# The last stage of a two-layer encoder trunk: the residual made token-major by 32-row reads and VectorE transposes instead of TensorE products with the identity

## The chip, the cores and the metric

The kernel runs on one core of a Trainium2 chip, in one launch. The metric is the device time of that launch in microseconds (us). The median of three runs of the kernel before is 1172.42 us (1171.95 to 1172.59). The profile shown below comes from one further execution, which took 1172.3 us; its profiled span is 1170.3 us, so some 2.0 us of an execution lie around the span.

## The reference

The reference is a trunk of two layers over 512 tokens of width 1024, in float32. Each layer is a token mixer, an output projection and a residual, then a gated MLP with a causal convolution, and a residual again. The change concerns only the very end: the down projection of the second layer's MLP (width 2816), its residual, and the final norm.

```python
def rmsnorm(x, g):
    x32 = x.astype(jnp.float32)
    y = x32 * lax.rsqrt(jnp.mean(x32 * x32, axis=-1, keepdims=True) + EPS)
    return (y * g.astype(jnp.float32)).astype(x.dtype)

def conv_ffn(h, w_up, conv_w, conv_b, w_down):
    u, g = jnp.split(h @ w_up, 2, axis=-1)
    g = causal_dwconv(g, conv_w, conv_b)
    return (jax.nn.silu(g) * u) @ w_down
...
for l in range(DEPTH):
    ...
    x = x + conv_ffn(rmsnorm(x, norm_ffn_g[l]), ffn_w_up[l], ffn_conv_w[l], ffn_conv_b[l], ffn_w_down[l])
return rmsnorm(x, final_g)
```

## The kernel before

**Layout.** Activations are kept feature-major: a tile has 128 features as partitions and the 512 tokens along the free axis, so the residual is eight tiles `xT[j]` of 128 x 512. Every float32 product is computed as three matmuls of rounded parts (`mm3`, lines 201 to 203): high by high, high by low, low by high. `split` (lines 145 and 146) makes the parts: ScalarE copies the rounded high part, VectorE subtracts to get the low part.

**The second MLP.** `ChannelMixer.tiles` walks over the 22 tiles of the hidden width. In each step it projects, convolves, gates, and `keep` stores the hidden tile as a pair `(hi, lo)`. The down projection of the first 16 hidden tiles is done inside these steps and added onto the residual in DRAM (`xspill`) by accumulating DMAs on the GpSimd queue. The last six hidden tiles (16 to 21) are left for the last stage. The steps are written in regions of `tc.manual_schedule`, in which TensorE, ScalarE and VectorE each issue their instructions in the written order; an instruction outside a region may be put anywhere between them by the scheduler.

**The last stage** (lines 1578 to 1657, outside any region). `channel_mixer` runs the steps and then `reload_x`, which issues eight reads of 128 x 512 (256 KB, rows of 2 KB) from `xspill` on the SyncE queue into the tiles `fh` and `fl`. The output must be token-major, 128 tokens as partitions, so here the hidden tile is the stationary operand: for each half `hf` of the 1024 output columns, for each pair `u` of hidden tiles (three pairs) and each of four token tiles `T`, TensorE runs 2 x 3 matmuls of 128 x 512 into one PSUM bank per `T`. `ws[u]` is the split pair of weights for `(hf, u)`, loaded into one of three `wr` buffers and split into one of three blocks `wh`/`wl`; the blocks of half 1 reuse those of half 0 when TensorE is through with them. In half 1 the token tiles come in groups: 0 and 1 together, then 2, then 3 in two pieces of 256 columns.

Between half 0 and half 1 stands `token_major(T, hf)`, eight times: four TensorE transposes of 128 x 128 (products with the identity `ident`, line 1590) turn a 128-token column block of four `xT` tiles into one PSUM bank, and a ScalarE copy (line 1592) brings it to SBUF as `xt[T][hf]`. Then `V.tensor_add` (line 1652) adds the product, `add_squares` sums the squares on ScalarE (line 1605), half 0 is multiplied by the final gain (line 1655), and `final_norm(T)` (lines 1607 to 1623) computes the root on ScalarE (line 1610), refines it on VectorE (1611 to 1614), scales both halves (1619 on ScalarE, 1620 on VectorE) and stores them (1621 on the SyncE queue, 1623 on ScalarE's).

The pool tag `pt` has two buffers of 10 KB per partition; in the second MLP they hold the raw weights and the weight sums of the steps (`ChannelMixer.buffers`).

Of the kernel before, what the change touches and what calls it, by code (L numbers as in the profile page):

```python
# [13 lines left out]
ALU = mybir.AluOpType  # L14
# [45 lines left out]
def trunk(  # L60
# [83 lines left out]
    def split(hi, lo, src, on_act=True, pinned=False):  # L144
        high = A.copy(hi, src) if on_act else V.tensor_copy(hi, src)  # L145
        low = V.tensor_tensor(out=lo, in0=src, in1=f(hi), op=ALU.subtract)  # L146
        if pinned:
            pin(high)
            pin(low)
# [3 lines left out]
    def load(src, a, b, extra=None):  # L153
        n = b + (extra.shape[-1] if extra is not None else 0)
        raw = sb("wr", [P, D])[:, : a * n].rearrange("p (a b) -> p a b", a=a)
        if isinstance(src, list):
            for i, one in enumerate(src):
                nc.sync.dma_start(raw[:, i, :], one)
        else:
            loads.append(nc.sync.dma_start(raw[:, :, :b], src))  # L160
        if extra is not None:
            nc.sync.dma_start(raw[:, :, b:], extra)
        return raw
# [28 lines left out]
    def weights(*args):  # L192
        return parts(load(*args))

    def rows(w, c0, n, k0=0, k1=None):
        k1 = k1 if k1 is not None else w.shape[0] // P
        return w[k0 * P : k1 * P, c0 : c0 + n].rearrange("(k p) c -> p k c", p=P)

    def mm3(o, lh, ll, rh, rl, first, last, more=False):

        nc.tensor.matmul(o, lh, rh, start=first, stop=False, skip_group_check=more)  # L201
        nc.tensor.matmul(o, lh, rl, start=False, stop=False, skip_group_check=more)  # L202
        nc.tensor.matmul(o, ll, rh, start=False, stop=last, skip_group_check=more)  # L203
# [537 lines left out]
    class ChannelMixer:  # L741
# [841 lines left out]
    for hf in range(2):  # L1583
        G.dma_start(fgb[hf], bass.AP(tensor=final_g.tensor, offset=final_g.offset + hf * S, ap=[[0, P], [1, S]]))
    xt = [[None] * 2 for _ in range(TT)]

    def token_major(T, hf):
        tp = ps("tr")
        for i in range(4):
            nc.tensor.transpose(tp[:, i * P : (i + 1) * P], xT[4 * hf + i][:, T * P : (T + 1) * P], ident)  # L1590
        xt[T][hf] = sb("u", [P, S])
        A.copy(xt[T][hf], tp)

    sums = [[] for _ in range(TT)]

    def add_squares(T, t):

        if len(sums[T]) == 1:
            V.tensor_scalar(sums[T][0], sums[T][0], 4.0 / D, 4 * EPS, op0=ALU.mult, op1=ALU.add)
        elif sums[T]:  # L1600
# [4 lines left out]
        A.activation(sq[:, : t.shape[-1]], t, AF.Square, accum_out=sums[T][-1])  # L1605

    def final_norm(T):
        v, r, t = small(1), small(1), small(1)
        first, second = sums[T]
        A.activation(r, second, AF.Sqrt, scale=4.0 / D, bias=first)  # L1610
        V.scalar_tensor_tensor(v, second, -4.0 / D, first, op0=ALU.mult, op1=ALU.subtract)
        V.reciprocal(r, r)
        V.scalar_tensor_tensor(t, r, v, r, op0=ALU.mult, op1=ALU.mult)
        V.scalar_tensor_tensor(r, t, 3.0, r, op0=ALU.add, op1=ALU.mult)
        step = S if T < TT - 1 else MEM
        for c in range(0, S, step):
            a, b = (t[:, c : c + step] for t in xt[T])
            last = c + step == S
            A.activation(a, a, AF.Copy, scale=r)
            V.scalar_tensor_tensor(b, b, r, fgb[1][:, c : c + step], op0=ALU.mult, op1=ALU.mult)  # L1620
            nc.sync.dma_start(out[T * P : (T + 1) * P, S + c : S + c + step], b)
            if last:
                nc.scalar.dma_start(out[T * P : (T + 1) * P, :S], xt[T][0])

    hid = channel_mixer(mixer)
    n = LAST // 2
    for hf in range(2):
        os_ = [ps(t) for t in (("mm", "mm", "mm", "sc") if hf == 0 else ("sc", "sc", "tr", "tr"))]
        ws = [None] * n
        groups = [(range(TT), (slice(0, S),))]  # L1630
        if hf:

            groups = [((0, 1), (slice(0, S),)), ((2,), (slice(0, S),)), ((3,), (slice(0, MEM), slice(MEM, S)))]
        for Ts, pieces in groups:
            for c in pieces:
                if c.start:
                    os_[Ts[0]] = ps("mm")
                for u in range(n):
                    if ws[u] is None:
                        k0 = FT - LAST + 2 * u  # L1640
                        ws[u] = weights(rows(ffn_w_down[1], hf * S, S, k0, k0 + 2), 2, S)
                    wh, wl = ws[u]
                    for T in Ts:
                        for i in range(2):
                            k = 2 * u + i
                            lh, ll = (t[:, T * P : (T + 1) * P] for t in hid[k])
                            mm3(os_[T][:, c], lh, ll, wh[:, i, c], wl[:, i, c], k == 0, k == LAST - 1)
                if not hf:
                    for i in range(KT):
                        token_major(i % TT, i // TT)  # L1650
                for T in Ts:
                    V.tensor_add(xt[T][hf][:, c], xt[T][hf][:, c], os_[T][:, c])
                    add_squares(T, xt[T][hf][:, c])
                    if hf == 0:
                        V.tensor_mul(xt[T][0], xt[T][0], fgb[0])
                    elif c.stop == S:
                        final_norm(T)


# [44 lines left out]
```

## Time and profile before

| what | value |
|---|---|
| runs, median of 3 (lowest, highest) | 1172.42 us (1171.95, 1172.59) |
| the profiled execution | 1172.3 us, span 1170.3 us, granted TensorE clock 0.999 |
| TensorE matmul busy | 1159.8 us, 99% of the span |
| VectorE busy | 992.1 us, 85% |
| ScalarE busy | 748.4 us, 64% |
| GpSimd busy | 151.6 us, 13% |
| HBM traffic | 149 GB/s over the span |

Times in the trace are microseconds from the start of the span. A row of the timeline gives the start, the duration, the engine, the line of the kernel, the operation, what it writes and reads by the program's names with the shape, how many were merged, and in brackets the idle time before it with what ended it. PE is TensorE's matmuls, PEld its weight loads, DVE VectorE, ACT ScalarE, SPq and ACTq the DMA queues of SyncE and ScalarE. The ends of matmuls are modelled and overlap the next one, so the pace of matmuls is read from the distance of their starts; on VectorE too an instruction overlaps the next by a little.

### The profile page before, as it was taken

The numbers are of one execution on the slowest core, as the hardware profiler recorded it, in microseconds if no ns is written. First come the engines' busy times: TensorE is split into PE (matmuls) and PEld (weight loads), VectorE is DVE, ScalarE is ACT, GpSimd is POOL, SyncE is SP. The second block draws the span as 40 slices with busy tenths as digits, with TensorE's granted clock in tenths as the row PEclk, the third lists the DMA queues.
The fourth block names the chain that finished last, engine by engine and source line by source line (L and its number), as shares of the span: only waits on it lengthen the run. The fifth ranks groups of instructions, "written<-read, shape, count | busy, mean of one in ns | idle before, by whom it ended". The sixth has DMA issues, their size and how long they took to land.

```text
span 1170.3 us, 19339 instructions
## 1 busy us (share of the span) xinstructions
PE 1159.8 (99%) x7221; PEld 1035.7 (88%) x7221; DVE 992.1 (85%) x1776; ACT 748.4 (64%) x1347; POOL 151.6 (13%) x254
## 2 busy tenths in 40 slices
PE   9999999999999999999999999999999999999997
PEld 9988888888999999999888888778899999999986
DVE  6777688779999988888798888898999998998865
ACT  6548677657766655555666667676766765556645
POOL 1211101000122222111020000101010111111100
PEclk9999999999999999999999999999999999999999
DMA  8745325244478888776573313335445677777661
GB/s 286 225 111 138 91 55 153 68 141 139 130 162 195 195 193 202 181 170 140 151 217 110 91 54 96 106 89 176 122 149 153 143 156 177 175 178 171 135 163 72
DMA packets 204784, 171.27 MB, mean 146 GB/s; under 512 B 9256, under 2 KB 177934, under 8 KB 204690
## 3 DMA queue, kind: packets, MB, share of 16 engines
q1 hardware_dynamic: 184946, 123.93, 36.3%
q0 software_dynamic: 19168, 45.06, 19.3%
q8 instruction: 56, 0.92, 0.3%
q10 hardware_dynamic: 576, 1.05, 0.2%
q14 instruction: 38, 0.31, 0.1%
HBM read 133.09 MB, written 40.85 MB: 149 GB/s over the span
## 4 chain that ended last, share of the span: by engine, by line
PE 95%; ACT 2%; DVE 2%; DMA 0%; issue 0%; SPq 0%; POOL 0%; POOLq 0%; DVEq 0%
PE pmm L201 18%; PE pmm L202 18%; PE pmm L203 18%; PE ptr L202 6%; PE ptr L201 6%; PE ptr L203 6%; PE psc L203 5%; PE psc L202 5%; PE psc L201 5%; PE psc L620 2%; PE ptr L1526 1%; PE ptr L1547 1%; PE ptr L1548 1%; PE ptr L689 0%; DMA u<-in_mem_dram 0%; PE pmm L511 0%
## 5 line engine op out<-in xcount | busy, mean ns | idle before, releaser
L201 PE MATMUL pmm<-u,wh 128*128 128x256 f32 (+1 forms) x992 | 334.7, 338 | 0.2 <-ACT u L145 0.2
L203 PE MATMUL pmm<-u,wl 128*128 128x256 f32 (+1 forms) x992 | 332.0, 335 | 0.0
L202 PE MATMUL pmm<-u,wh 128*128 128x256 f32 (+1 forms) x992 | 331.8, 334 | 0.0
L146 DVE TENSOR_TENSOR wl<-wr,wh 128x1024 fp32r<-128x1024 f32 (+4 forms) x166 | 186.1, 1121 | 67.4 <-ACT wh L145 66.9
L145 ACT CAST wh<-wr 128x1024 fp32r<-128x1024 f32 (+4 forms) x166 | 160.5, 969 | 68.0 <-PE pmm L202 30.0
L203 PEld LDWEIGHTS pmm<-u,wl 128*128 128x128 f32 x992 | 186.3, 188 | 18.8
L201 PEld LDWEIGHTS pmm<-u,wh 128*128 128x128 f32 x992 | 186.4, 188 | 16.8 <-ACT u L145 1.0
L202 PEld LDWEIGHTS pmm<-u,wh 128*128 128x128 f32 x992 | 186.5, 188 | 16.3 <-DVE u L146 0.5
L201 PE MATMUL ptr<-u,wh 128*128 128x512 f32 x272 | 106.5, 391 | 0.0
L202 PE MATMUL ptr<-u,wh 128*128 128x512 f32 x272 | 106.3, 391 | 0.0
L203 PE MATMUL ptr<-u,wl 128*128 128x512 f32 x272 | 105.8, 389 | 0.0
L145 ACT CAST fh<-pt 128x512 fp32r<-128x512 f32 x120 | 74.8, 625 | 34.5 <-DVE pt L1052 33.1
L201 PE MATMUL pmm<-u,fh 128*128 128x256 f32 x320 | 88.9, 278 | 0.0
L203 PE MATMUL pmm<-u,fl 128*128 128x256 f32 x320 | 88.6, 277 | 0.0
L974 ACT COPY t<-pmm 128x256 f32<-128x256 f32 x120 | 45.1, 376 | 67.9 <-PE pmm L203 67.9
L202 PE MATMUL pmm<-u,fh 128*128 128x256 f32 x320 | 88.5, 277 | 0.0
L146 DVE TENSOR_TENSOR fl<-pt,fh 128x512 fp32r<-128x512 f32 x120 | 82.2, 687 | 3.1
L763 DVE SCALAR_TENSOR_TENSOR t<-t,cols,t 128x511 f32<-128x511 f32 x88 | 65.9, 749 | 7.3 <-ACT t L770 5.8
L201 PE MATMUL psc<-u,wh 128*128 128x256 f32 (+1 forms) x208 | 63.2, 304 | 0.0
L203 PE MATMUL psc<-u,wl 128*128 128x256 f32 (+1 forms) x208 | 63.0, 303 | 0.0
L202 PE MATMUL psc<-u,wh 128*128 128x256 f32 (+1 forms) x208 | 62.9, 302 | 0.0
L201 PEld LDWEIGHTS pmm<-u,fh 128*128 128x128 f32 x320 | 60.1, 188 | 2.2 <-ACT t L974 0.7
(360 smaller groups left out, 2638.2 us busy)
## 6 DMA issues: line engine op xcount, KB each, us to landing
wr<-in_ffn_w_up_dram SPq DMA_DIRECT2D x46, 512.0 KB, 8.9
pt<-in_ffn_w_up_dram SPq DMA_DIRECT2D x40, 512.0 KB, 8.0
wr<-in_ffn_w_down_dram SPq DMA_DIRECT2D x32, 512.0 KB, 5.4
wr<-in_a_w_in_dram SPq DMA_DIRECT2D x20, 512.0 KB, 3.9
xspill<-bias POOLq DMA_DIRECT2D x32, 256.0 KB, 6.8
without_row<-bias POOLq DMA_DIRECT2D x24, 256.0 KB, 4.2
wr<-in_w_kv_dram SPq DMA_DIRECT2D x12, 512.0 KB, 3.8
without_row<-t POOLq DMA_DIRECT2D x24, 256.0 KB, 4.2
```

The costliest lines, as they stand in the source:

```text
L145: high = A.copy(hi, src) if on_act else V.tensor_copy(hi, src)
L146: low = V.tensor_tensor(out=lo, in0=src, in1=f(hi), op=ALU.subtract)
L201: nc.tensor.matmul(o, lh, rh, start=first, stop=False, skip_group_check=more)
L202: nc.tensor.matmul(o, lh, rl, start=False, stop=False, skip_group_check=more)
L203: nc.tensor.matmul(o, ll, rh, start=False, stop=last, skip_group_check=more)
L620: nc.tensor.matmul(o, a, b, start=first and i == 0, stop=i == 1)
L763: V.scalar_tensor_tensor(acc[:, n:], src[:, : S - n], self.fw[:, c * FT + j : c * FT + j + 1], acc[:, n:], op0=ALU.mult, op1=ALU.add,)
L974: A.copy(o, r[:, :H])
L1526: nc.tensor.transpose(tp[:, b * P : (b + 1) * P], es[T, h][:, b * P : (b + 1) * P], ident)
L1547: nc.tensor.matmul(o2[:, s * P :], w, hi_at(pts[h], s, s, TT - s), start=s == 0, stop=False)
L1548: nc.tensor.matmul(o2[:, s * P :], w, lo_at(pts[h], s, s, TT - s), start=False, stop=s == TT - 1)
```

## The change

- `reload_x` of the last stage is replaced by `load_quadrants`: two tiles `xq[hf]` in the `pt` buffers, each filled by four reads. A read takes 512 channels by 128 tokens and places them on 32 partitions: partition `32 b + p`, block `f`, column `t` holds channel `32 f + p` of the half and token `128 b + t`. A read has 512 runs of 512 bytes, 256 KB in all; there are eight, as there were eight before.
- `token_major(T, hf)` becomes one VectorE transpose of 128 x 512, which turns each 32 x 32 block by itself, and writes `xt[T][hf]` in SBUF. Its source takes every fourth column of `xq[hf]`. So the token tile `T` now holds the tokens `4 m + T`, with `m` the partition. No transposes on TensorE and no ScalarE copies remain.
- To match, `keep` orders the columns of the last six hidden tiles by `(T, m)`: both instructions of `split` read the source with a step of four elements. `out_rows` stores to rows `4 m + T`.
- The last stage is put in a region of `tc.manual_schedule`, with a written order: half 0 with `u` outermost; the weights of half 1 are split right after each `u` of half 0; the eight VectorE transposes stand after the split of `ws[0]` and ahead of that of `ws[1]`. The first two token tiles' additions of half 0 stand ahead of the split of `ws[2]`. In half 1 the order is `finished` of tiles 0 and 1, `root` of both, `norm_rows` of both, then tile 2, and `norm_rows(2)` behind the addition of the first piece of tile 3.
- The raw weights of half 1 and the eight reads stand in one order on the SyncE queue: weights 0, weights 1, the eight reads, weights 2.
- `final_norm` is cut into `root` and `norm_rows`; the small scaling of the first sum of squares moves ahead of half 1.

```diff
         def keep(self, t):
             hi, lo = sb("u", [P, S], F32R), sb("u", [P, S], F32R)
-            split(hi, lo, t)
+            if self.l and len(self.hid) >= FT - LAST:
+
+                a, b = (w.rearrange("p (T m) -> p T m", T=TT) for w in (hi, lo))
+                split(a, b, t.rearrange("p (m T) -> p T m", T=TT))
+            else:
+                split(hi, lo, t)
...
-    def channel_mixer(mixer):
+    def channel_mixer(mixer, reload=reload_x):
         mixer.tiles()
-        reload_x()
+        reload()
...
+    B = 32
+    xq = []
+
+    def load_quadrants():
+
+        for hf in range(2):
+            xq.append(sb("pt", [P, 5 * S])[:, : 4 * S].rearrange("p (f t) -> p f t", t=P))
+            for b in range(4):
+                block = xspill[4 * hf][:, b * P :]
+                src = bass.AP(tensor=block.tensor, offset=block.offset, ap=[[S, B], [B * S, 16], [1, P]])
+                tc.keep_in_program_order(nc.sync.dma_start(xq[hf][b * B : (b + 1) * B], src))
+
+    def out_rows(T, c0, n):
+        return out.rearrange("(m t) c -> t m c", t=TT)[T][:, c0 : c0 + n]
 
     def token_major(T, hf):
-        tp = ps("tr")
-        for i in range(4):
-            nc.tensor.transpose(tp[:, i * P : (i + 1) * P], xT[4 * hf + i][:, T * P : (T + 1) * P], ident)
         xt[T][hf] = sb("u", [P, S])
-        A.copy(xt[T][hf], tp)
+        block = xq[hf].rearrange("p f (c t) -> p f c t", t=TT)[:, :, :, T]
+        V.transpose(xt[T][hf].rearrange("p (f c) -> p f c", c=B), block)
...
+    def raw_weights(hf, u):
+        k0 = FT - LAST + 2 * u
+        return load(rows(ffn_w_down[1], hf * S, S, k0, k0 + 2), 2, S)
+
+    def reload():
+        ws.extend(parts(raw_weights(0, u)) for u in range(n))
+        for u in range(n):
+            raws.append(raw_weights(1, u))
+            pin(loads[-1])
+            if u == 1:
+                load_quadrants()
...
+    with tc.manual_schedule(engines=ORDERED):
+        os_ = [ps(t) for t in ("mm", "mm", "mm", "sc")]
+        for u in range(n):
+            multiply(os_, range(TT), whole, u)
+            if u == n - 1:
+                for T in range(2):
+                    finished(os_[T], T, 0, whole)
+            ws[u] = parts(raws[u])
+            if not u:
+                for i in range(2 * TT):
+                    token_major(i % TT, i // TT)
+        for T in range(2, TT):
+            finished(os_[T], T, 0, whole)
+        for T in range(TT):
+            V.tensor_mul(xt[T][0], xt[T][0], fgb[0])
+            V.tensor_scalar(sums[T][0], sums[T][0], 4.0 / D, 4 * EPS, op0=ALU.mult, op1=ALU.add)
+        os_ = [ps(t) for t in ("sc", "sc", "tr", "tr")]
+        for u in range(n):
+            multiply(os_, (0, 1), whole, u)
+        for step in (finished_whole, root, norm_rows):
+            for T in range(2):
+                step(T)
+        for u in range(n):
+            multiply(os_, (2,), whole, u)
+        finished_whole(2)
+        root(2)
+        for c in (slice(0, MEM), slice(MEM, S)):
+            if c.start:
+                os_[3] = ps("mm")
+            for u in range(n):
+                multiply(os_, (3,), c, u)
+            finished(os_[3], 3, 1, c)
+            if not c.start:
+                norm_rows(2)
+        root(3)
+        norm_rows(3)
```

`multiply` is the loop of `mm3` over the given token tiles for one `u`; `finished` is the addition and `add_squares`.

More of the change, by code (lines that the diff above doesn't have):

```diff
@@ L1605, in add_squares, with root @@
         A.activation(sq[:, : t.shape[-1]], t, AF.Square, accum_out=sums[T][-1])
-    def final_norm(T):
-        v, r, t = small(1), small(1), small(1)
+    roots = [None] * TT
+    def root(T):
+        v, r = small(1), small(1)
         first, second = sums[T]
@@ L1611, in final_norm, with norm_rows @@
         V.scalar_tensor_tensor(v, second, -4.0 / D, first, op0=ALU.mult, op1=ALU.subtract)
+        roots[T] = v, r
+    def norm_rows(T):
+        (v, r), t = roots[T], small(1)
         V.reciprocal(r, r)
@@ L1620, in final_norm @@
             V.scalar_tensor_tensor(b, b, r, fgb[1][:, c : c + step], op0=ALU.mult, op1=ALU.mult)
-            nc.sync.dma_start(out[T * P : (T + 1) * P, S + c : S + c + step], b)
+            nc.sync.dma_start(out_rows(T, S + c, step), b)
             if last:
-                nc.scalar.dma_start(out[T * P : (T + 1) * P, :S], xt[T][0])
-    hid = channel_mixer(mixer)
+                nc.scalar.dma_start(out_rows(T, 0, S), xt[T][0])
     n = LAST // 2
[L1627 to L1657, printed above, removed]
```

19 lines of the change are left out of this document (16 added, 3 removed).

## The prediction

> **What bounds the kernel now.** I read the page's first lines and its chain, then the timeline of each engine from 1120 us to the end.
>
> ```profile
> PE 1159.8 (99%) x7221; PEld 1035.7 (88%) x7221; DVE 992.1 (85%) x1776; ACT 748.4 (64%) x1347; POOL 151.6 (13%) x254
> ...
> PE 95%; ACT 2%; DVE 2%; DMA 0%; issue 0%; SPq 0%; POOL 0%; POOLq 0%; DVEq 0%
> ```
>
> TensorE is the bound: 95% of the chain is matmuls. So work taken off TensorE is worth its time, until another engine sets the end. The place of the change in TensorE's timeline:
>
> ```profile
> 1141.82 0.40 PE L203 MATMUL psc<-wh,u 128*128 128x512 f32 x1
> 1142.06 1.04 PE L1590 MATMUL ptr<-ident,fh 128*128 128x128 f32 x8
> 1142.85 0.48 PE L201 MATMUL psc<-wh,u 128*128 128x512 f32 x1
> ...
> 1154.54 0.39 PE L201 MATMUL ptr<-wh,u 128*128 128x512 f32 x1
> ...
> 1158.62 0.28 PE L201 MATMUL ptr<-wh,u 128*128 128x256 f32 x1
> ...
> 1160.78 0.28 PE L201 MATMUL pmm<-wh,u 128*128 128x256 f32 x1
> ...
> 1162.82 0.28 PE L203 MATMUL pmm<-wh,u 128*128 128x256 f32 x1
> ```
>
> The first row is the last matmul of half 0, the last row the last of half 1. Token tile 2 is the 18 matmuls from 1154.54 to 1158.62, so a 128x512 matmul takes a pace of 4.08 / 18 = 0.227; the first piece of tile 3 gives 2.16 / 18 = 0.120 for 128x256. The transposes (L1590) stand among the matmuls of tiles 0 and 1 of half 1. What they bring to the other engines:
>
> ```profile
> L1592 ACT COPY u<-ptr 128x512 f32<-128x512 f32 x8 | 4.5, 588 | 0.4 <-PE ptr L1590 0.3
> ...
> L1590 PE MATMUL ptr<-ident,fh 128*128 128x128 f32 x16 | 2.3, 276 | 0.1
> ```
>
> VectorE around it, and ScalarE's cast of the last weights:
>
> ```profile
> 1132.69 1.23 DVE L146 TENSOR_TENSOR wl<-wr,wh 128x1024 fp32r<-128x1024 f32 x1 [0.26 <-ACT wh L145]
> 1137.90 1.23 DVE L146 TENSOR_TENSOR wl<-wr,wh 128x1024 fp32r<-128x1024 f32 x1 [3.98 <-ACT wh L145]
> 1143.34 1.23 DVE L146 TENSOR_TENSOR wl<-wr,wh 128x1024 fp32r<-128x1024 f32 x1 [4.22 <-ACT wh L145]
> 1144.48 1.88 DVE L1652 TENSOR_TENSOR u<-u,pmm 128x512 f32<-128x512 f32 x3
> ...
> 1149.80 0.69 DVE L1655 TENSOR_TENSOR u<-u,bias 128x512 f32<-128x512 f32 x1 [0.34 <-ACT t L1605]
> ...
> 1150.47 0.68 DVE L1655 TENSOR_TENSOR u<-u,bias 128x512 f32<-128x512 f32 x1
> ```
> ```profile
> 1142.26 1.05 ACT L145 CAST wh<-wr 128x1024 fp32r<-128x1024 f32 x1 [4.40 <-PE psc L203]
> ```
>
> VectorE idles 4 us twice during half 0. Three 128x512 operations in a row take 1.88, so each comes 0.60 behind the one before ((1.88 - 0.68) / 2); a 128x1024 one takes a pace of 1.14 (1143.34 to 1144.48); a multiplication by the gain with its small operation 0.67 (1149.80 to 1150.47).
>
> **The change part by part.**
>
> *The 32 transposes leave TensorE.* Without them half 1 begins 0.227 behind the row at 1141.82, at 1142.05. Tiles 0 to 2 are 54 x 0.227 = 12.24, so tile 3 begins at 1154.29 and not at 1158.62: 4.33 us gained. This contains the waits between transposes and copies too. Eight ScalarE copies go (4.5 us); they were beside the matmuls and are counted at nothing more.
>
> *Eight VectorE transposes come.* No row shows one. The nearest is the 128x512 operation at a pace of 0.60 with contiguous operands. The source here takes every fourth element; if that halves the reading, the nearest row is the one with twice the elements, 1.14. Below 0.60 a transpose could only help, and it would not show, as the sum will say. I take 0.60, since the element count is the same, and keep 1.14 for a rival. They stand behind the low part of ws[0] (1132.69 + 1.14 = 1133.83) and end at 1133.83 + 8 x 0.60 = 1138.63. Behind them in VectorE's written order: the low part of ws[1] to 1139.77 (TensorE wants it after 12 matmuls of half 1, at 1144.77), the first two additions to 1140.97 with ScalarE's squares to about 1141.8, the cast of ws[2] at 1142.26 as before (it waits for half 0 to end), its low part from 1143.34 to 1144.48 (wanted at 1142.05 + 24 x 0.227 = 1147.5), two additions to 1145.68, four gain pairs of 0.67 to 1148.36. Tile 0 of half 1 is complete at 1142.05 + 29 x 0.227 + 0.39 = 1149.0. So all of it fits. The reserve is small: 0.44 until the squares push the cast, 0.64 ahead of tile 0, and about 0.8 between tiles 0 and 1: 1.9 us together.
>
> *The written order of the tail.* Before, the tail ran like this:
>
> ```profile
> 1153.38 0.69 DVE L1652 TENSOR_TENSOR u<-u,psc 128x512 f32<-128x512 f32 x1 [2.17 <-PE psc L203]
> ...
> 1156.47 0.16 DVE L1612 RECIPROCAL s<-s 128x1 f32<-128x1 f32 x1 [0.97 <-ACT s L1610]
> ...
> 1157.11 0.75 DVE L1620 SCALAR_TENSOR_TENSOR u<-u,s,bias 128x512 f32<-128x512 f32 x1
> 1157.78 0.15 DVE L1611 SCALAR_TENSOR_TENSOR s<-s,s 128x1 f32<-128x1 f32 x1
> ...
> 1160.97 0.42 DVE L1652 TENSOR_TENSOR u<-u,ptr 128x256 f32<-128x256 f32 x1 [0.92 <-PE ptr L203]
> 1161.31 0.15 DVE L1611 SCALAR_TENSOR_TENSOR s<-s,s 128x1 f32<-128x1 f32 x1
> ...
> 1163.13 0.42 DVE L1652 TENSOR_TENSOR u<-u,pmm 128x256 f32<-128x256 f32 x1 [0.29 <-PE pmm L203]
> ```
> ```profile
> 1154.11 0.63 ACT L1605 ACTIVATE t<-u 128x512 f32<-128x512 f32 x1 [3.73 <-DVE u L1652]
> ...
> 1154.85 1.28 ACT L1610 ACT_TABLE_LOAD   x1
> 1156.14 0.29 ACT L1610 ACTIVATE s<-s,s 128x1 f32<-128x1 f32 x1
> ```
>
> The last addition (1163.13) followed the last matmul at once. Steps read from these rows: addition to square 0.73, square to the next on ScalarE 0.74, table load 1.29, root to reciprocal 0.33, reciprocal to scaling 0.64, scaling to the next 0.67. Before, the table load stood between the squares of tiles 0 and 1; now both squares come first, so it starts later. Tile 1 is complete at 1142.05 + 35 x 0.227 + 0.39 = 1150.4. From there: square 1151.13, table load 1151.87, root 1153.16, scaling of tile 0 at 1154.13, of tile 1 at 1155.44, addition of tile 2 at 1156.11 (its product was there at 1154.5), its root at 1157.58; behind that VectorE's small operation and the first addition of tile 3 (1157.74), then 0.34 + 0.64 to the scaling of tile 2 (1158.72) and 0.67 to the last addition: 1159.39. TensorE is done at 1154.29 + 35 x 0.120 + 0.28 = 1158.77. The order costs 0.6 us that before was hidden. What follows the last addition has the same operations and stores of the same size, counted as equal.
>
> *The reads.* Eight of 256 KB as before, now in runs of 512 bytes into 32 partitions.
>
> ```profile
> 1121.60 0.38 SPq L160 DMA_DIRECT2D wr<-in_ffn_w_down_dram  x1
> ...
> fl<-xspill SPq DMA_DIRECT2D x4, 256.0 KB, 3.2
> ...
> DMA to landing us min/median/max: 3.8/8.1/13.0
> ```
>
> The first row is the load of weights 1 of half 1; it waits for its buffer, and the reads stand right behind it, so they are issued from about 1121.98. Weights 2 are queued behind them; eight issues of some 0.4 us end by 1125.7, and nobody wants these weights before 1142.26. Nearest rows: the old reads landed in 3.2 with four under way (the second row), so eight end by about 1131. The loads of the up weights, also in runs of 512 bytes, took 3.8 at best and 8.1 at the median for 512 KB (the third row, of that tensor), much of it beside accumulating DMAs that are over by then. Four such in a row at the best are 15.2, landing at 1137.2; the last four transposes would then end at 1137.2 + 2.4 = 1139.6, 1 us late, inside the reserve. I take the price as nothing, with the median (32 us, landing at 1154.4) as the far end.
>
> *The strided splits of the last six hidden tiles.*
>
> ```profile
> 1123.99 0.62 ACT L145 CAST u<-t 128x512 fp32r<-128x512 f32 x1
> ```
>
> At worst ScalarE goes from 0.62 to the 1.05 of the 1024-element cast, VectorE from 0.60 to 1.14. Five of the six lie in steps with products queued; tile 21's is needed only by the last third of half 0. Taken as nothing, at most 0.5.
>
> *Sum.* The last addition moves from 1163.13 to 1159.39: 3.74 us. On the profiled execution 1172.3 - 3.7 = 1168.6; the median stands 0.1 higher, so 1168.7. A measurement of this kernel can tell about 0.2%, 2.3 us, from no change.
>
> The Trainium skill has a rule against this change: "SBUF — State Buffer", Door 1, says that SBUF lines are 16 bytes and that each access that goes to a new line pays a penalty. A step of four float32 is exactly one line per element. No run here shows its price; with the pace of 1.14 the sum would be the rival next below.
>
> **Rivals.**
>
> *Half-rate transposes.* At 1.14 they end at 1142.95; the low part of ws[1] at 1144.09, additions to 1145.29, the square 1146.14 now pushes the cast of ws[2], its low part ends at 1148.36 (TensorE waits 0.6 for it), additions 1149.56, gain pairs 1152.24, tile 1 added at 1152.84 instead of 1150.40. The tail moves with it: last addition 1161.83, gain 1.3: 1171.1. For it: the reserve of 1.9 is less than the 4.3 that it costs. Against it: no row shows strided reading slower.
>
> *The fill is lost.*
>
> ```profile
> 1122.69 0.40 PE L201 MATMUL pmm<-wh,u 128*128 128x512 f32 x1
> ...
> 1124.15 0.38 PE L201 MATMUL pmm<-u,fh 128*128 128x256 f32 x1
> ...
> 1125.68 0.40 PE L201 MATMUL pmm<-wh,u 128*128 128x512 f32 x1
> ...
> 1126.38 0.28 PE L201 MATMUL psc<-u,fh 128*128 128x256 f32 x1
> ```
>
> Nine matmuls of half 0 (six, then three) run inside two waits of the last hidden step. If the new region kept them behind that step, 9 x 0.227 = 2.0 us come back: 1170.7. Against it: a region orders only its own instructions.
>
> *Late reads, and slower.* The written order puts the transposes ahead of the split of ws[1], the additions and the split of ws[2]; if the reads land late, all that waits, and past the reserve each us is paid in full. The gain is gone when the transposes end 3.74 + 1.9 = 5.6 late, at 1144.3: the second half landing at 1141.9, 20 us after the first issue. At 6 us for each 512 KB, between the 3.8 and the 8.1 above, it lands at 1146: 4.1 us slower, 1176.5. For it: 8.1 is the median of such runs. Against it: the old reads, of the same size and with four under way, landed in 3.2.
>
> By the same page of the Trainium skill a transfer into 32 partitions reaches half the ports, 189 GB/s at 1 MiB; that is an estimate of 11 us for these 2.1 MB, inside the reserve.
>
> *More gain.* If the tail's 0.6 stays hidden: 1168.1; and the new store pattern may shift the last landing by a us, to 1167.0.
>
> **How the numbers follow.** The sum 0.46 (own range 1167.9 to 1169.9), half-rate transposes 0.20, fill lost 0.08, late reads 0.17, more gain 0.09. I predict 1168.7. The range goes from 1167.0, the best case, to 1173.0, which takes in half-rate and lost fill and leaves out most of the late reads. Faster: the first and the last and a quarter of the two between, 0.60; within 0.2%: 0.21; slower: late reads and a little, 0.19.
>
> **What the changed profile would show.** Right: no transposes between the halves, half 1 starting 0.23 behind half 0's last matmul, VectorE's transposes near 0.69 each and done before 1140, the last addition about 0.6 behind the last matmul. Half-rate: transposes near 1.2, TensorE waiting for a low part, the last addition 2 us or more behind. Late reads: VectorE idle ahead of a transpose with a DMA as releaser. Fill lost: TensorE idle near 1123 and 1126. I am wrong above all if VectorE, in one fixed order, turns out to have less reserve than 1.9 us.

## The result and the profile after

| | before | after |
|---|---|---|
| median, us (lowest, highest) | 1172.37 (1171.95, 1173.03) | 1169.99 (1169.49, 1170.49) |
| the profiled execution, us (span) | 1172.3 (1170.3) | 1169.64 (1167.5) |

Both rows of runs were taken on one chip, 12 of each. The ratio is 0.9979, with an interval from 0.9970 to 0.9988: 2.4 us faster. Forecast were 1168.7 and a gain of 3.7, so the gain is 1.3 us short.

The first lines of the page of after, and its chain:

```profile
PE 1155.7 (99%) x7189; PEld 1032.8 (88%) x7189; DVE 1001.4 (86%) x1784; ACT 747.1 (64%) x1339; POOL 151.3 (13%) x254
...
PE 92%; DVE 4%; ACT 3%; issue 1%; DMA 0%; SPq 0%; POOL 0%; DVEq 0%; POOLq 0%; ACTq 0%
```

TensorE's share of the chain fell from 95% to 92%, and VectorE's rose from 2% to 4%. The chain in order of time shows where (start, us, piece; "issue" is time in which the engine waited for nothing that the profile shows):

```profile
1122.18 0.13 PE pmm L202
...
1122.33 1.05 ACT wh L145
...
1123.64 1.04 ACT u L145
...
1124.71 1.10 DVE u L146
...
1131.05 1.10 ACT u L145
...
1140.17 2.03 DVE u L1609 x2
```

The first row is the last piece of TensorE. The other 45 us are ScalarE and VectorE up to the last store, through the strided splits of hidden tiles 20 and 21 (the three rows with `u` and L145 or L146) and the transposes (L1609). Before, nearly all of the chain up to the last matmul was TensorE's. TensorE's timeline at the places that the prediction named:

```profile
1122.24 0.40 PE L201 MATMUL pmm<-wh,u 128*128 128x512 f32 x1
...
1127.73 0.39 PE L201 MATMUL pmm<-wh,u 128*128 128x512 f32 x1
...
1141.81 0.39 PE L203 MATMUL psc<-wh,u 128*128 128x512 f32 x1
1142.03 0.39 PE L201 MATMUL psc<-wh,u 128*128 128x512 f32 x1
...
1158.46 0.28 PE L203 MATMUL pmm<-wh,u 128*128 128x256 f32 x1
```

The first row is the first of the nine fill matmuls inside the last hidden step, here called the mark; in before it stood at 1122.69. Its start differs by up to 1.1 us between profiles of kernels that are alike up to there (1122.22 in split_first_table_early and 1123.33 in contiguous_turn, two of the experiments below), so times of two profiles are compared from this mark. The second row is where half 0 goes on without a gap. Half 1 starts 0.22 behind half 0: the transposes are gone from TensorE. VectorE in the same stretch, and ScalarE:

```profile
1134.32 7.88 DVE L1609 STREAM_TRANSPOSE u<-pt 128x512 f32<-128x512 f32 x8
1142.10 1.21 DVE L146 TENSOR_TENSOR wl<-wr,wh 128x1024 fp32r<-128x1024 f32 x1
1143.20 1.31 DVE L1669 TENSOR_TENSOR u<-u,pmm 128x512 f32<-128x512 f32 x2
1146.25 1.23 DVE L146 TENSOR_TENSOR wl<-wr,wh 128x1024 fp32r<-128x1024 f32 x1 [1.75 <-ACT wh L145]
...
1151.24 1.27 DVE L1669 TENSOR_TENSOR u<-u,psc 128x512 f32<-128x512 f32 x2
...
1160.74 0.41 DVE L1669 TENSOR_TENSOR u<-u,pmm 128x256 f32<-128x256 f32 x1
```
```profile
1143.94 0.63 ACT L1620 ACTIVATE t<-u 128x512 f32<-128x512 f32 x1 [6.09 <-DVE u L1669]
...
1145.18 1.04 ACT L145 CAST wh<-wr 128x1024 fp32r<-128x1024 f32 x1
...
1153.31 1.28 ACT L1627 ACT_TABLE_LOAD   x1
```

This is a queue in which each piece waits for the one before. The transposes end at 1142.10, which is 19.86 behind the mark; forecast was 1138.63, 15.94 behind the mark of before. Behind them stand the low part of `ws[1]` and the first two additions; ScalarE idles 6.09 us for the first of these, squares both, and only then casts the last weights (1145.18; before 1142.26). Their low part follows at 1146.25 (before 1143.34), then additions and gain multiplications, and token tile 1 of half 1 is added by the second of the two operations at 1151.24. The table load starts at 1153.31 instead of the 1151.87 forecast, and the last addition comes 1160.74 - 1158.46 - 0.28 = 2.00 behind the end of the last matmul. TensorE never waits for any of this, though the low part of `ws[2]` is done at 1147.48, some 0.2 us ahead of the first matmul that reads it; it simply finishes first.

From the mark to the last addition before took 1163.13 - 1122.69 = 40.44 and after takes 38.50: 1.94 gained. From there to the end of the span it is 7.17 and 6.76, another 0.41. Together 2.35, against 2.38 between the medians. That the two are so near is chance: the profiled execution of after was itself 0.35 below its median.

### The profile page after: what moved, and what is told of

It is laid out like the page before. It is cut to its first block, busy times and chain, and to the rows that moved or that the text cites. A ratio compares the mean times of both kernels' runs of the same rounds, so it can differ in the third digit from the quotient of the medians.

```text
span 1167.5 us, 19279 instructions
## 1 busy us (share of the span) xinstructions
PE 1155.7 (99%) x7189; PEld 1032.8 (88%) x7189; DVE 1001.4 (86%) x1784; ACT 747.1 (64%) x1339; POOL 151.3 (13%) x254
## 3 DMA queue, kind: packets, MB, share of 16 engines
q10 hardware_dynamic: 576, 1.05, 0.2%
## 4 chain that ended last, share of the span: by engine, by line
PE 92%; DVE 4%; ACT 3%; issue 1%; DMA 0%; SPq 0%; POOL 0%; DVEq 0%; POOLq 0%; ACTq 0%
PE pmm L201 18%; PE pmm L202 18%; PE pmm L203 18%; PE ptr L202 6%; PE ptr L201 6%; PE ptr L203 6%; PE psc L203 4%; PE psc L202 4%; PE psc L201 4%; PE psc L620 2%; PE ptr L1531 1%; PE ptr L1552 1%; PE ptr L1553 1%; DVE u L1609 1%; PE ptr L689 0%
## 5 line engine op out<-in xcount | busy, mean ns | idle before, releaser
L146 DVE TENSOR_TENSOR wl<-wr,wh 128x1024 fp32r<-128x1024 f32 (+4 forms) x166 | 185.9, 1120 | 57.6 <-ACT wh L145 57.1
L145 ACT CAST wh<-wr 128x1024 fp32r<-128x1024 f32 (+4 forms) x166 | 160.5, 969 | 62.6 <-PE pmm L202 30.0
L145 ACT CAST fh<-pt 128x512 fp32r<-128x512 f32 x120 | 74.8, 625 | 34.5 <-DVE pt L1057 33.2
L146 DVE TENSOR_TENSOR fl<-pt,fh 128x512 fp32r<-128x512 f32 x120 | 82.2, 687 | 3.1
```

## Experiments

In all of them the number that tells most is the stretch from the mark to the last addition: 40.44 before, 38.50 after. The diffs are against the changed kernel unless said otherwise. Each ratio is to runs of the kernel before on the same chip. The experiments ran on four chips, on which before's medians lie between 1171.89 and 1172.40, so a difference of a few tenths between two experiments is read from their stretches rather than from their medians.

**1. Transposes with contiguous sources (contiguous_turn).**

```diff
-        block = xq[hf].rearrange("p f (c t) -> p f c t", t=TT)[:, :, :, T]
+        block = xq[hf][:, :, T * B : (T + 1) * B]
```

> Only the source of VectorE's eight transposes changes: each reads 32 neighbouring columns of a block instead of every fourth (the residual then belongs to other tokens). Theory: the step of four elements is what makes a transpose take 1.07 us, and the tail pays for it. Then a transpose takes about 0.69 at a pace of 0.60, the eight end near 1139.1 instead of 1142.1, the last addition comes about 0.6 behind the last matmul instead of 2.0, and the median falls by 1.2 to 1.5 us, to about 1168.6. Rival: 1.07 is what a transpose takes whatever its source; then nothing changes.

Measured: 1168.54 us, ratio to before 0.9967 [0.9954, 0.9979]. The group of the transposes in this kernel's trace (shortest, median and longest in ns, first and last start):

```profile
L1609 DVE STREAM_TRANSPOSE u<-pt x8: 667/668/700, 1135.4 to 1139.6; 128x512 f32<-128x512 f32 x8
```

and in after's:

```profile
L1609 DVE STREAM_TRANSPOSE u<-pt x8: 1040/1068/1082, 1134.3 to 1141.1; 128x512 f32<-128x512 f32 x8
```

The step of four costs 0.40 us in each. The eight become 3.0 us shorter together, but the stretch only 1.46 (37.04): the other half was hidden. The last addition now comes 0.55 behind the end of the last matmul instead of 2.00.

**2. Each transpose twice (twice_turned).**

```diff
-        V.transpose(xt[T][hf].rearrange("p (f c) -> p f c", c=B), block)
+        for _ in range(2):
+            V.transpose(xt[T][hf].rearrange("p (f c) -> p f c", c=B), block)
```

> Every VectorE transpose is done twice (the second writes the same again): 7.8 us more on VectorE. Theory: nothing of VectorE's reserve is left, so 7 to 8 us are paid in full, partly as TensorE waiting for the low parts of the weights of half 1: about 1177.5. Rival: VectorE has idle time there that hides some of it; then 1.5 us or more below that, under 1176.

Measured: 1179.08 us, ratio 1.0056 [1.0042, 1.0070], 9.1 us more than after. The row of the transposes, and of the waits:

```profile
1134.88 16.79 DVE L1610 STREAM_TRANSPOSE u<-pt 128x512 f32<-128x512 f32 x16
```
```profile
PE psc L202 <- DVE wl L146: 7.2, 1, 7.2
```

The median is 1.6 us above the 1177.5 expected, because the sixteen take 1.05 us each and not 0.97 (why is not shown), so the edit adds 8.9 us of VectorE time; the stretch grows by 8.92 (to 47.42). So what is added on VectorE ahead of the second weights is paid in full: the changed kernel has no reserve left. TensorE itself now waits 7.2 us for the low part of `ws[1]`, but the chain that ends last still runs over VectorE.

**3. The splits ahead of the additions (split_first), and the table load early (split_first_table_early).**

```diff
+            ws[u] = parts(raws[u])
             if u == n - 1:
                 for T in range(2):
                     finished(os_[T], T, 0, whole)
-            ws[u] = parts(raws[u])
...
+        A.preload_act_table_set("sqrt_and_others")
         os_ = [ps(t) for t in ("sc", "sc", "tr", "tr")]
```

The line with `preload_act_table_set` is in the second kernel alone.

> The split of the last weights of half 1 stands ahead of the first two additions of half 0 in the written order, instead of behind them. Theory: the tail is late because ScalarE's cast of these weights stands behind two squares that wait for VectorE's additions, and VectorE then idles 1.75 us for the cast. Then the cast starts near 1142.2 instead of 1145.2, the idle time goes, the last addition comes 0.6 behind the last matmul, and the median falls by 1.2 to 1.5 us, to about 1168.6, with the transposes as slow as before. Rival: the tail is late for another reason (the stores, the reads); then less than 0.3.

> As split_first, and the table for the root is loaded on ScalarE right behind half 0's last squares, where ScalarE idles, instead of behind the squares of tiles 0 and 1. Theory: what is left of the tail's delay is the 1.3 us of that load; the last addition then follows the last matmul at once (1158.8) and the median is 0.5 to 0.7 below split_first, about 1168.0. Rival: the delay is in the order of VectorE's steps; then as split_first.

Measured: split_first 1168.67 us, ratio 0.9967 [0.9955, 0.9980], stretch 37.02; with the table early 1167.89 us, 0.9963 [0.9949, 0.9976], stretch 36.53. VectorE of the second:

```profile
1134.30 7.87 DVE L1609 STREAM_TRANSPOSE u<-pt 128x512 f32<-128x512 f32 x8
1142.10 2.42 DVE L146 TENSOR_TENSOR wl<-wr,wh 128x1024 fp32r<-128x1024 f32 x2
1144.43 1.88 DVE L1669 TENSOR_TENSOR u<-u,pmm 128x512 f32<-128x512 f32 x3
...
1158.75 0.42 DVE L1669 TENSOR_TENSOR u<-u,pmm 128x256 f32<-128x256 f32 x1 [0.42 <-PE pmm L203]
```

The transposes are as long as in after. Since the additions no longer stand ahead of ScalarE's cast, both low parts run back to back at 1142.10 and the second is done 3.0 us earlier (2.42 behind 1142.10, against 1.23 behind 1146.25); of that 1.48 arrives at the last addition in split_first, where the last addition comes 0.55 behind the end of the last matmul. With the table load out of the tail, VectorE waits for TensorE again at the last addition (the bracket in the last row): nothing is left between the last matmul and it.

**4. Contiguous transposes once more, with that order (sfte_contig).** The edit of experiment 1 on split_first_table_early.

> Edit on top of split_first_table_early: the transposes read 32 tokens in a row instead of every fourth (the residual of other tokens is added). The same edit on the changed kernel took 1.45 us. Theory: there it paid because the second weights' splits stood behind additions that stood behind the transposes; with the splits ahead VectorE has a reserve again, the transposes' price (1.07 or 0.67 us each) is hidden, and the time stays within 0.3 us of 1167.9. Rival: some other work behind the transposes still waits for them, and another 1 us or more is gained: 1166.9 or below.

Measured: 1167.85 us, ratio 0.9961 [0.9948, 0.9975], against 1167.89; stretch 36.55 against 36.53. The same 3.0 us of VectorE work that gave 1.5 in experiment 1 give nothing here:

```profile
1137.29 2.49 DVE L1609 STREAM_TRANSPOSE u<-pt 128x512 f32<-128x512 f32 x4 [0.32 <-DMA pt<-xspill]
1139.71 1.18 DVE L146 TENSOR_TENSOR wl<-wr,wh 128x1024 fp32r<-128x1024 f32 x1
1143.50 1.23 DVE L146 TENSOR_TENSOR wl<-wr,wh 128x1024 fp32r<-128x1024 f32 x1 [2.61 <-ACT wh L145]
```

They turn into idle time: 2.61 us ahead of the low part of `ws[2]`, which waits for ScalarE's cast and with it for half 0 to end. So the transposes' price mattered only through the written order behind them. (The first row shows the second four waiting 0.32 us for the reads.)

**5. TensorE transposes in the written order (tensor_turn).** Region, early weights and tail as in the change; but the residual is read in plain rows and turned by TensorE with copies by ScalarE, the splits are contiguous, the token order plain.

```diff
...
-        V.transpose(xt[T][hf].rearrange("p (f c) -> p f c", c=B), block)
+        tp = ps("tr")
+        for i in range(4):
+            nc.tensor.transpose(tp[:, i * P : (i + 1) * P], xq[hf][:, 4 * i + T, :], ident)
+        A.copy(xt[T][hf], tp)
...
-            if not u:
+            if u == 1:
```

> The written order, the early weights and the split norm stay; the residual is again read in 128-partition rows and turned by 32 TensorE transposes and eight ScalarE copies (tokens in their own order, no strided splits). In the order the transposes stand behind the split of the second weights. Theory: the gain is TensorE's time for the transposes, so without it the time is that of the kernel before or above it, 1172.4 to 1174. Rival: the gain comes from the written order and the early weights; then it stays near 1170.

Measured: 1173.53 us, ratio 1.0012 [1.0003, 1.0020]; stretch 42.07. TensorE's rows of its transposes, and where half 0 goes on:

```profile
1136.47 1.04 PE L1603 MATMUL ptr<-ident,pt 128*128 128x128 f32 x8
1138.26 1.15 PE L1603 MATMUL ptr<-ident,pt 128*128 128x128 f32 x8 [0.75 <-ACT u L1604]
...
1141.82 0.48 PE L201 MATMUL pmm<-wh,u 128*128 128x512 f32 x1
```

The transposes stand in one block here and take 5.35 us, 1.0 more than the 4.33 in before, with 1.13 us of waiting for ScalarE's copies; the last matmul is 1.12 later from the mark than in before (41.25 against 40.13), and the last addition comes 0.54 behind its end. These two account for all of the 1.63 by which the stretch is longer than before's. So even without that waiting the order alone gains nothing: the change gains only when the transposes leave TensorE.

**6. VectorE transposes without the written order (free_order).** Before's last stage, outside any region, with the 32-row reads and the VectorE transposes, and with the strided splits and the output rows that go with them.

> The kernel before with VectorE's transposes and the 32-row reads alone: no written order, the norm in one piece, the weights of half 1 where they were. Theory: TensorE's 4.3 us are gained here too, and the scheduler keeps the table load early; 1168.5 to 1170.5. Rival: without the written order VectorE's queue delays the low parts or the additions and the gain is lost; 1172 or more.

Measured: 1176.22 us, ratio 1.0031 [1.0020, 1.0043]: slower than before. I had expected it near the changed kernel, and that theory fell. VectorE's and TensorE's timelines of this kernel:

```profile
1141.40 4.03 DVE L1608 STREAM_TRANSPOSE u<-pt 128x512 f32<-128x512 f32 x4
1145.37 1.24 DVE L1671 TENSOR_TENSOR u<-u,bias 128x512 f32<-128x512 f32 x2
1146.54 0.67 DVE L1668 TENSOR_TENSOR u<-u,psc 128x512 f32<-128x512 f32 x1
1147.13 1.21 DVE L146 TENSOR_TENSOR wl<-wr,wh 128x1024 fp32r<-128x1024 f32 x1
```
```profile
1143.23 0.73 PE L201 MATMUL psc<-wh,u 128*128 128x512 f32 x2 [1.11 <-ACT wh L145]
...
1148.39 0.80 PE L202 MATMUL psc<-wl,u 128*128 128x512 f32 x1 [3.97 <-DVE wl L146]
```

The scheduler placed the last four transposes, two gain multiplications and an addition ahead of the low part at 1147.13. TensorE waits 3.97 us for it, and 1.11 for a cast of the weights of half 1: more than the 4.33 that it was freed of. That is not all of the loss:

```profile
1149.41 0.63 PE L201 MATMUL psc<-wh,u 128*128 128x512 f32 x1
...
1151.97 0.52 PE L202 MATMUL psc<-wl,u 128*128 128x512 f32 x1
```

Behind the long wait the matmuls come 0.427 us apart (2.56 for six) instead of 0.227, with a granted clock of 0.50 from 1148.4 to 1152.0. The ten steps from the end of the wait at 1148.39 to 1152.33 take 3.94 instead of 2.27 us, which is 1.67 more. From the last matmul of half 0 to the last of all TensorE takes 24.09 us here and 16.65 in after; the two waits and the slower pace are 6.75 of the 7.44. So the stall cost TensorE more than its own length. The written order is a condition of the gain.

**7. Contiguous splits of the last hidden tiles (plain_splits).** The products are then those of other tokens.

```diff
-            if self.l and len(self.hid) >= FT - LAST:
-                a, b = (w.rearrange("p (T m) -> p T m", T=TT) for w in (hi, lo))
-                split(a, b, t.rearrange("p (m T) -> p T m", T=TT))
-            else:
-                split(hi, lo, t)
+            split(hi, lo, t)
```

> Only the splits of the last six hidden tiles read contiguously again (the products then belong to other tokens than the residual). Theory: they are hidden, because the half 0 matmuls that fill the last hidden step take up the waits; within 0.3 us of the changed kernel. Rival: the 0.4 us that each of the two instructions takes longer are paid where a product waits for them; then 0.4 us or more faster.

Measured: 1168.90 us, ratio 0.9971 [0.9960, 0.9982], 1.1 us faster than after. I had held the splits to be worth 0.3 at most; the rival was right. In after a strided split takes, on ScalarE and on VectorE,

```profile
1123.54 1.14 ACT L145 CAST u<-t 128x512 fp32r<-128x512 f32 x1
```
```profile
1124.71 1.10 DVE L146 TENSOR_TENSOR u<-t,u 128x512 fp32r<-128x512 f32 x1
```

against 0.62 on ScalarE in before and 0.69 on VectorE in the contiguous form (the row is from experiment 9). Two things follow. TensorE's mark-to-resumption takes 1127.73 - 1122.24 = 5.49 in after, while before it took, with this row of before,

```profile
1127.74 0.40 PE L201 MATMUL pmm<-wh,u 128*128 128x512 f32 x1
```

1127.74 - 1122.69 = 5.05, and in plain_splits also 5.05: TensorE loses 0.44. And the longer splits delay VectorE's queue, those of tile 20 by 0.5 us and those of tile 21 by another 0.5: the split of tile 21 on VectorE starts 9.94 behind the mark in after and 8.99 in plain_splits, the transposes 12.08 and 11.08. In both kernels the last addition comes well behind TensorE's end (2.00 and 1.43), so it is VectorE's 1.0 that is paid here (the stretch is 37.50), and TensorE's 0.44 lies inside it.

**8. That loss by order (step_order).** On split_first_table_early, VectorE's addition that frees the accumulator buffer TensorE waits for stands ahead of the split of tile 20, in the last hidden step.

```diff
-            then(tail, "split")
+            ends = self.l and j == FT - 1
+            if not ends:
+                then(tail, "split")
             then(first, "split_up")
             V.tensor_tensor(out=new.pre[:, H:], in0=new.u3[:, :H], in1=new.r3[:, :H], op=ALU.add)
+            if ends:
+                then(tail, "split")
```

> Edit on top of split_first_table_early: in the last hidden step of layer 1 VectorE's addition into the next operand (the one that reads the accumulator buffer which TensorE needs next) is issued ahead of the split of hidden tile 20 instead of behind it. Theory: the slower strided split (1.10 us in place of 0.69) costs TensorE 0.44 us in this step only because it stands ahead of that addition; with the addition ahead the step takes 5.05 us or less from the first fill product to the resumption in place of 5.49, and the time falls from 1167.9 to about 1167.4. Rival: TensorE waits in this step for something else that ends as late (ScalarE's casts, or tile 20's parts for its down products), and the time stays at 1167.9 within 0.3 or rises.

Measured: 1167.64 us, ratio 0.9960 [0.9948, 0.9973], against 1167.89 and 0.9963: 0.25 less, on another chip, which the runs can't tell from nothing. Its TensorE rows:

```profile
1122.98 0.40 PE L201 MATMUL pmm<-wh,u 128*128 128x512 f32 x1
...
1127.39 0.39 PE L201 MATMUL pmm<-wh,u 128*128 128x512 f32 x1
```

The step takes 4.41, with six fill matmuls instead of nine; the three that now follow it are 0.69, so 0.38 is won, and the stretch shows 0.39 (36.14). The trace bears the theory out; the medians only allow it.

**9. The stride in TensorE's weight loads (strided_loads).** On split_first_table_early, contiguous splits; the stationary operand takes every fourth column.

```diff
...
-                lh, ll = (t[:, T * P : (T + 1) * P] for t in hid[k])
+                lh, ll = (t.rearrange("p (m T) -> p T m", T=TT)[:, T] for t in hid[k])
```

> Edit on top of split_first_table_early: the last six hidden tiles are split as all others are, contiguously, and the last stage's weight loads of TensorE read every fourth column of them instead. Theory: the strided access moves to a place where it is hidden, a load of 188 ns beside a matmul pace of 227 ns, as long as it lengthens by less than 39 ns; then the two splits are back at 0.69 us on VectorE and 0.62 us on ScalarE, the last hidden step is back at 5.05 us, and the time is about 1167.4. Rival: the strided load lengthens as VectorE's split did (by 0.4 to 0.6 of itself, to 270 to 300 ns), loads set the pace of the stage, and its some 140 to 290 matmuls cost 5 us or more: 1173 or above.

Measured: 1173.08 us, ratio 1.0006 [0.9997, 1.0015]: the rival. Groups of weight loads in the last stage, first this kernel, then after:

```profile
L203 PEld LDWEIGHTS psc<-wh,u 128*128 128x128 f32 x18 | 5.6, 310 | 0.0
```
```profile
L203 PEld LDWEIGHTS psc<-wh,u 128*128 128x128 f32 x18 | 3.4, 188 | 0.7
```

TensorE's rows of the last token tile in this kernel, and the contiguous split on VectorE that experiment 7 used:

```profile
1161.95 0.39 PE L202 MATMUL pmm<-wl,u 128*128 128x256 f32 x1
...
1163.59 0.39 PE L203 MATMUL pmm<-wh,u 128*128 128x256 f32 x1
```
```profile
1125.04 0.69 DVE L146 TENSOR_TENSOR u<-t,u 128x512 fp32r<-128x512 f32 x1
```

A load takes 310 ns instead of 188; it overlaps the next, and loads follow each other every 0.234 us ((1163.59 - 1161.95) / 7). For the 126 matmuls of 128x512 that is 0.007 more than their own pace; for the 36 of 128x256, whose pace was 0.120, it is 0.114 more. 0.9 + 4.1 = 5.0 of the 5.2 us by which this kernel is slower than split_first_table_early. The load is hidden behind a wide matmul and is the pace of a narrow one.

**10. The reads in 128 partitions (wide_reads).** The same bytes in rows of 2 KB; the residual then lies in other places.

```diff
-                src = bass.AP(tensor=block.tensor, offset=block.offset, ap=[[S, B], [B * S, 16], [1, P]])
-                tc.keep_in_program_order(nc.sync.dma_start(xq[hf][b * B : (b + 1) * B], src))
+                tc.keep_in_program_order(nc.sync.dma_start(xq[hf][:, 4 * b : 4 * b + 4], xspill[4 * hf + b].rearrange("p (f t) -> p f t", t=P)))
```

> The eight reads bring the same bytes as rows of 2 KB into 128 partitions (the residual is then no longer the transposed one). Theory: the reads land before VectorE comes to their transposes, so the time stays within 0.3 us, while the reads land in 3 to 4 us each instead of 8.4. Rival: they hold something up (the last weights behind them, or a transpose); then 0.5 us or more faster.

Measured: 1170.09 us, ratio 0.9981 [0.9972, 0.9989], as after. The reads in after and then in wide_reads (the last number is us from issue to landing):

```profile
pt<-xspill SPq DMA_DIRECT2D x8, 256.0 KB, 8.4
```
```profile
pt<-xspill SPq DMA_DIRECT2D x8, 256.0 KB, 5.2
```

The 32-row form takes 8.4 us at the median and not 5.2 (expected were 3 to 4 for the wide one), and nobody waits for either: after's transposes start at 1134.32 right behind the split ahead of them and run on without a gap.

**11. A step of two instead of four (step_two).**

```diff
-        block = xq[hf].rearrange("p f (c t) -> p f c t", t=TT)[:, :, :, T]
+        block = xq[hf].rearrange("p f (c t) -> p f c t", t=2)[:, :, T // 2 * B : (T // 2 + 1) * B, T % 2]
```

> Edit on the changed kernel: the eight transposes read every second token instead of every fourth (a step of 8 bytes instead of 16; the residual of other tokens is added). Theory, by what the Trainium skill says in "SBUF — State Buffer", Door 1 (lines of 16 bytes, two accesses to a line are enough): a transpose costs as much as the contiguous one, 0.67 us in place of 1.07, and the time is that of contiguous_turn, about 1168.5. Rival: any step costs, in proportion to the bytes that it skips or in full: a transpose takes 0.8 to 1.07 us and the time lies between 1169 and 1170.

Measured: 1168.47 us, ratio 0.9968 [0.9956, 0.9980], like contiguous_turn. The group of its transposes:

```profile
L1609 DVE STREAM_TRANSPOSE u<-pt x8: 665/670/711, 1135.2 to 1140.0; 128x512 f32<-128x512 f32 x8
```

670 ns: a step of 8 bytes costs nothing, a step of 16 costs 0.40 us. That is what the Trainium skill's line rule says ("SBUF — State Buffer", Door 1: two accesses to a line of 16 bytes are enough); the trace agrees, and puts the price at 60% of the transpose.

## Why the prediction was right, and where it was off

**The 32 transposes: 4.33 forecast, 3.91 measured.** From the mark, the last matmul moved from 40.13 to 36.22. The mechanism is right: there is no gap between the halves, and experiment 5 shows that the order without this gains nothing, experiment 6 that this without the order gains nothing either. The missing 0.42 is not in this term but in the strided splits: in plain_splits the last matmul is at 35.79, 4.34 earlier than in before.

**The strided splits: forecast nothing, at most 0.5.** This step failed. It looked at the products queued in the steps, not at what stands behind a split on VectorE. The splits cost TensorE 0.44 in the last hidden step and delay VectorE's queue by 1.0, and it is the second that is paid: the medians of experiment 7 put it at 1.1 us. The bound for one instruction (1.05 and 1.14) was about right (1.14 and 1.10).

**The transposes' pace: 0.60 taken, 0.97 measured** (7.78 us for eight), between the ends 0.60 and 1.14. The contiguous row was the wrong one to be nearest to: the element count is the same, but the price followed the step (experiments 1 and 11), and the rule cited against the change was the better guide. This term was mis-sized by 8 x 0.37 = 3.0 us.

**The reserve: 1.9 us.** Its size was good. Against the forecast VectorE's transposes ended 19.86 - 15.94 = 3.9 late, 3.0 from the pace and the rest from the splits; the last addition is late by 38.50 - 36.70 = 1.80 (36.70 being the forecast 1159.39 less the mark), so 2.1 were hidden. With contiguous transposes the stretch is 37.04, and less the 0.42 of the hidden step 36.62, which is near the forecast; that is a sum, as no run takes both strides away in this order.

**The order of the tail: 0.6 forecast, 2.00 measured.** The chain was the one described, squares, table load, root, scaling; it started later by the terms above. Where VectorE is not late, the 0.6 comes out: the last addition is 0.55 behind TensorE's end in contiguous_turn and in split_first. So the other 1.45 is lateness, and either shorter transposes or a better order takes it away; the 0.55 is the table load, which the second kernel of experiment 3 moves out of the tail.

**The reads: right, but with little to spare.** No transpose of after waits for them. They landed at about 1137.1: in sfte_contig, whose mark (1122.41) is 0.17 later than after's, a transpose waited for them until 1137.29. Forecast was 1137.2, from four times 3.8, and that the two agree so well is partly luck: the rate was above those 138 GB/s (512 KB in 3.8 us), and weights moved beside the reads. After's DMA from 1126 to 1136, where most packets are the reads' 512 bytes:

```profile
DMA packets 3678, 1.93 MB, mean 193 GB/s; under 512 B 115, under 2 KB 3611, under 8 KB 3677
```

The Trainium skill gives 189 GB/s at 1 MiB for a transfer into 32 partitions ("SBUF — State Buffer", Door 1), and the trace agrees. The estimate of 11 us worked out from it came out short: the reads took some 15.4 us from the first issue at 1121.69, since 2.82 MB and not 2.1 moved from 1121 to 1136, weights among them.

**The fill: right.** Nine matmuls still run inside the last hidden step.

**Behind the last addition** equal cost was forecast; it is 0.41 less in after. In free_order and tensor_turn it is 6.76 and 6.78 as well, the first with before's order of the tail and the second with plain rows, so it needs neither the new order nor the new rows. Before has one profile here; whether its 7.17 is usual stays open.

Together: 3.74 - 1.80 + 0.41 = 2.35. The last 0.41 is luck as far as the prediction goes: nothing in it foresaw that. The rival nearest to the truth was the half-rate one, as the pace went two thirds of its way: counted from before's mark, the last addition came at 1161.19, between 1159.39 and 1161.83.

The best version found is step_order, 0.9960 [0.9948, 0.9973], or without its last edit 0.9963 [0.9949, 0.9976]: the change, with the splits ahead of the additions and the table load ahead of half 1.

## What to carry to other kernels

Work moved off the bounding engine is worth its time only as long as the written order of the engine that takes it has room: put what the bound needs, here the splits, and what the tail needs, here the table load, ahead of what can wait, before shaving the moved work itself. Price a strided float32 operand by how many of its elements share a line: a step of two was free in the transposes, a step of four made each pass over 512 elements 0.4 to 0.5 us longer on VectorE and ScalarE. A longer weight load is hidden only while the matmul beside it takes about as long as the load's pace (0.227 against 0.234 at 128x512), so a layout that suits the vector engines has to be priced at the narrowest matmul too.

## What the runs showed of the hardware that was not expected

- A transpose of 128x512 float32 on VectorE by 32 x 32 blocks costs as much as an addition of that shape when its source is contiguous or has a step of two (0.67 us), and 1.07 with a step of four.
- Weight loads with a step of four take 310 ns instead of 188, but follow each other every 0.234 us, so they overlap; at 128x512 they cost next to nothing.
- TensorE came back from its two longest waits at about half pace. In free_order it waited 3.97 us; the granted clock was 1.00 up to 1145.4, 1 us into the wait, and 0.50 from then to 1152.0. In twice_turned it waited 7.20 us, and the clock was 0.50 from 1152.8 to 1156.4. No other run waited longer than 0.75 us in this stage, and all of them show 1.00 from 1122 to 1158. Which length of wait brings it on is not shown.
- The reads into 32 partitions held back their own queue. Issues of the same queue in after, in ns (shortest, median, longest):

```profile
L1601 SPq DMA_DIRECT2D pt<-xspill x8: 346/850/2479, 1121.7 to 1128.9; - x8
```

In wide_reads the longest was 468 ns. From the first issue to the end of the last the queue took 8.62 us in after and 4.18 in wide_reads, and the load behind the reads was issued some 4 us later for it; nobody waited for that here.
